# Gate and up products with the weights stationary and the tokens streaming, in the second round of two feed-forwards

## The chip, the cores and the metric

The kernel runs on one core of a Trainium2 chip. The metric is the device time of one execution in microseconds (us); the time of a kernel is the median of its runs. All data is float32 in HBM; 256 tokens with 2048 channels go through one layer of an encoder.

## The reference

One layer has three residual parts: a feed-forward, a mixing part (attention and convolution) and a second feed-forward. Each part normalizes its input, scales and shifts it with vectors computed from a conditioning vector `c` ("modulation"), and normalizes its result again before it is added. What the change touches is the feed-forward:

```python
def swiglu(h, w_gate, w_up, w_down):
    return (jax.nn.silu(h @ w_gate) * (h @ w_up)) @ w_down

h = modulate(rms_norm(x, ffn1_pre_g[l]), sh1, sc1)        # 256 x 2048
f = swiglu(h, ffn1_w_gate[l], ffn1_w_up[l], ffn1_w_down[l])  # 2048 -> 5632 -> 2048
x = x + 0.5 * g1[:, None, :] * rms_norm(f, ffn1_post_g[l])
```

The second feed-forward is the same with its own weights. `mod = c_act @ w_ada + b_ada` gives the nine modulation vectors; `w_ada` alone has 151 MB.

## The kernel before

**Products.** Every operand of a large product is held as two parts of type float32r, a rounded one (hi) and the rest (lo), and a product is three matmuls: hi x hi, hi x lo, lo x hi. A weight chunk is two K tiles (2 x 128 rows) by 512 columns, 512 KB. `wchunk` issues its load on SyncE's queue into one of 7 `raw` buffers, ScalarE casts it to `hi` (L286), VectorE subtracts to get `lo` (L287); `hi` and `lo` have 4 buffers each. The input `hT` is stored transposed, channels on partitions and tokens along the free axis, so that it can be the stationary operand: `Group.products` takes 128 tokens of a K tile as the stationary side and streams 512 weight columns, the result being 128 tokens by 512 columns in one PSUM bank per token tile `t` (L312 to L314).

**Feed-forward.** The 5632 hidden columns are 11 blocks of 512, in two rounds: six blocks, then their share of the down product, then five blocks, then the rest of the down product. The first round (`ffn_start`) has its K tiles in stages, since the modulation is still being computed. The second round (`ffn_rest`, `th` = 1) calls `ffn_up` for each of its five blocks: the gate product `pg` (16 K tiles, 8 chunks), SiLU on ScalarE into `gs` (L446), the up product `pu`, their product `ac` on VectorE (L428). The activations then have their tokens on partitions, but the down product needs them transposed as a stationary operand. So `act_out` turns them: two deferred steps (`turn`, 2 and 3 weight chunks later) each put four 128x128 transposes on TensorE (L385, into a PSUM tile `pa`), a cast on ScalarE (L360) and a subtraction on VectorE (L361) into the two parts of `aT`.

**What sets the order.** The program is written out chunk by chunk: after each chunk's products `tick()` advances the deferred steps and the background lanes (modulation vectors: loads of `w_ada`, multiply-adds on VectorE at L190, transposes `psc` on TensorE at L204). Engines run their queues in order. PSUM has six banks for products (three pairs) and two for transposes. `ffn_down` reads `aT` as the stationary operand, chunk by chunk; the block that comes last is read in the last two of ten chunks.

Of the kernel before, what the change touches and what calls it, by code (L numbers as in the profile page):

```python
# [9 lines left out]
F32 = mybir.dt.float32  # L10
F32R = mybir.dt.float32r
AF = mybir.ActivationFunctionType
# [24 lines left out]
# Chunks over which token tile 0 runs ahead of tile 1 at a part's start and end, and K tiles of  # L37
# tile 0's input that come before the rest.
# [3 lines left out]
# Steps of background work per weight chunk: convolution, modulation in the first feed-forward  # L42
# and in the mixing part.
# [3 lines left out]
# Chunks between an elementwise result and its transposes: rope, activations, conv input.  # L47
# [3 lines left out]
# Buffers for chunks as loaded, and for each of their two parts.  # L51
# [3 lines left out]
# K tiles of the first products of each feed-forward, by stages of their modulation.  # L55
# [5 lines left out]
def encoder_layer(ctx, tc, a, consts, out):  # L61
# [15 lines left out]
    def mm_ps(name):  # L77
        return [psum.tile([P, BLK], F32, tag="mm", name=f"{name}_t{t}") for t in range(NT)]
# [63 lines left out]
    def load_cols(names, i):  # L142
        """Parameter vectors with element j*128+p at [p, j]."""
        rows = work.tile([P, P], F32, tag="rows", name=f"rows{i}")
        at = 0
        for name in names:
            n = a[name].shape[1] // P
            nc.gpsimd.dma_start(rows[at:at + n, :], a[name].rearrange("o (j p) -> (o j) p", p=P))
            pcols[name] = (at, n, i)
            at += n  # L150
        prm = keep.tile([P, sum(a[n].shape[1] for n in names) // P], F32, name=f"prm{i}")
        ps = tr_ps(f"ps_prm{i}")
        nc.tensor.transpose(ps[:, :at], rows[:at, :], ident[:at, :at])
        nc.scalar.copy(prm[:, :at], ps[:, :at])
        pcols[i] = prm
# [12 lines left out]
    def mod_sum(vs, c0, n):  # L168
        """Partial sums over the partitions of columns c0..c0+n of the vectors vs."""
        both = mpool.tile([P, MW], F32, tag="acc", name=f"acc{vs[0]}_{c0}")  # L170
        nc.gpsimd.memset(both, 0.0)
        accs = []
        for m, v in enumerate(vs):
            n0 = v * D + c0
            acc = both[:, m * n:(m + 1) * n]
            nc.gpsimd.dma_start(acc[0:1, :], b_ada[0:1, n0:n0 + n])
            accs.append(acc)
        kt = CH * BLK // n
        for j0 in range(0, NK, kt):
            ws = []  # L180
            for v in vs:
                n0 = v * D + c0
                raw = wpool.tile([P, CH, BLK], F32, tag="raw", bufs=RAW, name=f"ada{v}_{c0}_{j0}")
                w = raw.rearrange("p a b -> p (a b)").rearrange("p (j n) -> p j n", n=n)
                nc.sync.dma_start(w, w_ada[j0 * P:(j0 + kt) * P, n0:n0 + n].rearrange(
                    "(j p) n -> p j n", p=P))
                ws.append(w)
            for j in range(kt):
                for w, acc in zip(ws, accs):
                    nc.vector.scalar_tensor_tensor(acc, w[:, j, :], cact[:, j0 + j:j0 + j + 1], acc,  # L190
                                                   op0=ALU.mult, op1=ALU.add)
            for v in vs:
                yield
        return accs

    def mod_cols(vs, dsts, c0, n):
        """Columns c0..c0+n of the vectors vs with element j*128+p at dst[p, j]."""
# [17 lines left out]
    def mod_affine(vsh, vsc, gname, A, B, c0, n):  # L215
        """A = (1 + scale) * pre gain, B = shift, for columns c0..c0+n."""
# [9 lines left out]
    def mod_gate(v, gname, factor, gc):  # L226
        """gc = factor * vector v * post gain."""
# [4 lines left out]
    def gate_tile(gc, i):  # L232
        """The column vector gc as a row, the same on every partition."""
# [11 lines left out]
    def slot(tag, shape, name, dt=F32):  # L245
        """A tile of at most SLOT elements in a place that several parts use in turn."""
# [29 lines left out]
    def wchunk(w, r0, kt, cols, name):  # L276
        """K tiles from row r0 on, of 512 columns in equal parts from each of cols on."""
# [12 lines left out]
    class Group:  # L290
        """ps[t] (+)= x[t] @ w over K tiles k0..k0+nk and 512 columns; xT holds the K tiles
        from kx on."""
# [23 lines left out]
    def in_step(work):  # L316
        """Chunks of groups, all of token tile 0 before token tile 1."""
# [7 lines left out]
    def group(*args, head=0, tail=0, **kw):  # L325
        """A group, token tile 0 ahead of tile 1 over the first head and the last tail chunks."""
# [10 lines left out]
    def rstd_parts(ssp, n, name, act=False):  # L337
        """(sum of the columns of ssp / n + EPS) ** -0.5"""
# [24 lines left out]
    def pre_norm(hT, dg, A, B, j0, j1, i, t0=0, t1=NT):  # L363
        """K tiles j0..j1 of modulate(rms_norm(x)) transposed, for token tiles t0..t1; dg
        holds 1/rms on diagonals."""
# [15 lines left out]
    def transposed(src, ps, n=2):  # L381
        """[P tokens, t, n*128] -> PSUM [128, n, S]."""
# [17 lines left out]
    def post_add(f, r, i, t):  # L400
        """x += f * r for token tile t, r the rstd of the rows before the gain; returns 1/rms
        of the new rows on a diagonal."""
# [7 lines left out]
    def next_norm(f, ssp, A, B, j1, i):  # L410
        """Residual, and the first j1 K tiles of the next part's input, token tile 0 first over
        the chunks of a group's head."""
# [27 lines left out]

    def ffn_up(aT, slot_i, hT, wg, wu, b, i):
        pg = mm_ps(f"pg{i}_{b}")
        group(pg, hT, wg, 0, NK, b * BLK, f"g{i}_{b}")
        gs = gs_tile(f"{i}_{b}")
        for t in range(NT):
            nc.scalar.activation(gs[:, t, :], pg[t], AF.Silu)  # L446
        pu = mm_ps(f"pu{i}_{b}")
        group(pu, hT, wu, 0, NK, b * BLK, f"u{i}_{b}")
        act_out(aT, slot_i, gs, pu, f"{i}_{b}")
# [16 lines left out]
    def ffn_start(hT, wg, wu, i, stages, mods_of, norm_of, last_lane, begin=None):  # L466
        """Blocks of the first round, K tiles in stages: a stage's modulation is summed up
        while the products of the stage before run."""
# [64 lines left out]
    # ================= first feed-forward =================  # L533
# [35 lines left out]
    def begin2(open_group, run, order):  # L569
        """The first two groups with token tile 0 ahead."""  # L570
# [24 lines left out]
    # ================= attention and convolution =================  # L595
# [42 lines left out]
    def rope_T(pt, name, tag):  # L638
        """PSUM t x [P, 4 heads x 128] -> rotated and transposed [128, head, S]."""
# [26 lines left out]
    def attention(hb, qT, kT):  # L666
        """Heads of one half in overlapping steps: scores, transpose, output."""
# [58 lines left out]
    def attn_parts(hb, hi, lo):  # L726
        """Attention rows times their gain, transposed; 1/rms is applied after the product."""
# [30 lines left out]
    # layer norm over channels, swish: sums over channels on the tensor engine  # L758
# [9 lines left out]
    def rstd_cols(ps, n, name):  # L768
        """Sums of [128 equal rows, S tokens] -> 1/rms with the tokens on partitions."""
# [115 lines left out]
    # ================= second feed-forward =================  # L885
# [67 lines left out]
```

## Time and profile before

| | |
|---|---|
| median of 3 runs | 1992.02 us |
| lowest, highest | 1987.54, 1992.28 us |
| profiled execution, span from first to last instruction | 1997.8 us |
| TensorE busy | 1917.2 us (96%), 8547 matmuls |
| weight loads of TensorE | 1552.7 us (78%) |
| VectorE busy | 1466.7 us (73%) |
| ScalarE busy | 936.7 us (47%) |
| HBM read | 489 MB, 246 GB/s over the span |
| second round, first feed-forward (gate and up) | 465 to 697 us of the span |
| second round, second feed-forward (gate and up) | 1641 to 1871 us of the span |

In the profile's rows, PE is TensorE's matmuls and PEld its loads of stationary operands, ACT is ScalarE, DVE VectorE. `L312` is line 312 of the kernel, which made the instruction. Names are `out<-in`, without buffer numbers; `128*128 128x512` is a matmul with a 128x128 stationary operand and 512 streamed columns. Matmuls are pipelined: the profile's record of one goes on while the next has begun, so the distance between starts says how fast they go. A plain float32 matmul of the program appears as two records.

### The profile page before, as it was taken

The page shows a single profiled execution, that of the slowest core. Times are in us where ns is not written, and L with a number is a line of the kernel's source. Part 1 is how long each engine was busy: PE and PEld are TensorE (multiplying, and loading weights), DVE is VectorE, ACT ScalarE, POOL GpSimd, SP SyncE. Part 2 cuts the span into 40 slices and gives each one's busy share as a digit, 9 for nine tenths or more (in the row PEclk, how much of TensorE's full clock was granted, in tenths as well). Part 3 has the DMA queues.
Part 4 walks back from the last instruction along what each step waited for, and adds up shares of the span by engine and source line. Part 5 has one row for each costly group of instructions (what it writes and reads, how often), then busy time and mean ns, then how long its engine had stood idle before and what let it go on. Part 6 is the DMA issues. An engine that isn't in the chain of part 4 may idle for free.

```text
span 1997.8 us, 23978 instructions
## 1 busy us (share of the span) xinstructions
PE 1917.2 (96%) x8547; PEld 1552.7 (78%) x8547; DVE 1466.7 (73%) x1780; ACT 936.7 (47%) x1439; POOL 65.5 (3%) x90
## 2 busy tenths in 40 slices
PE   2999999999999999899999997999999999999997
PEld 2888888888888877678888786888888777888886
DVE  6789999777777766589997758898776455444454
ACT  3554455444444444644455745635444433444442
POOL 2000000000000000000100000000000000000000
PEclk9999999999999999899999998999999999999999
DMA  9989988999999977356656667998777667656552
GB/s 341 313 296 307 318 266 280 344 320 327 313 318 322 301 251 262 104 176 184 179 167 203 195 205 243 329 325 278 245 224 234 216 231 236 198 180 186 172 189 96
DMA packets 249432, 493.13 MB, mean 247 GB/s; under 512 B 17065, under 2 KB 42433, under 8 KB 249312
## 3 DMA queue, kind: packets, MB, share of 16 engines
q1 hardware_dynamic: 247888, 491.38, 73.8%
q8 instruction: 67, 1.10, 0.2%
q14 instruction: 53, 0.43, 0.1%
q0 software_dynamic: 1248, 0.15, 0.1%
q10 hardware_dynamic: 176, 0.07, 0.0%
HBM read 489.44 MB, written 2.10 MB: 246 GB/s over the span
## 4 chain that ended last, share of the span: by engine, by line
PE 85%; DMA 7%; DVE 4%; issue 2%; ACT 1%; POOL 0%; DVEq 0%; POOLq 0%; ACTq 0%; SPq 0%
PE pg_t L312 8%; PE pg_t L313 8%; PE pg_t L314 8%; PE pu_t L313 8%; PE pu_t L314 7%; PE pu_t L312 7%; DMA ada<-in_w_ada 7%; PE pd_t L313 6%; PE pd_t L314 6%; PE pd_t L312 6%; PE pc_t L312 2%; PE pc_t L313 2%; PE pc_t L314 2%; PE pst L374 1%; DVE lo_d L287 1%
## 5 line engine op out<-in xcount | busy, mean ns | idle before, releaser
L190 DVE SCALAR_TENSOR_TENSOR acc<-ada,cact,acc 128x512 f32<-128x512 f32 (+2 forms) x448 | 394.2, 900 | 148.4 <-DMA ada<-in_w_ada 138.0
L286 ACT CAST hi_d<-raw_d 128x1024 fp32r<-128x1024 f32 x176 | 184.4, 1050 | 273.6 <-PE pd_t L314 233.8
L286 ACT CAST hi_g<-raw_g 128x1024 fp32r<-128x1024 f32 x176 | 184.8, 1051 | 241.4 <-PE pg_t L314 143.8
L287 DVE TENSOR_TENSOR lo_d<-raw_d,hi_d 128x1024 fp32r<-128x1024 f32 x176 | 212.7, 1223 | 111.1 <-ACT hi_d L286 110.7
L286 ACT CAST hi_u<-raw_u 128x1024 fp32r<-128x1024 f32 x176 | 184.7, 1050 | 219.3 <-PE pu_t L314 121.7
L287 DVE TENSOR_TENSOR lo_u<-raw_u,hi_u 128x1024 fp32r<-128x1024 f32 x176 | 214.3, 1223 | 95.9 <-ACT hi_u L286 95.3
L287 DVE TENSOR_TENSOR lo_g<-raw_g,hi_g 128x1024 fp32r<-128x1024 f32 x176 | 214.4, 1223 | 77.1 <-ACT hi_g L286 76.7
L313 PE MATMUL pd_t<-lo_d,a_0h 128*128 128x512 f32 x384 | 152.3, 397 | 4.3 <-DVE lo_d L287 4.2
L312 PE MATMUL pd_t<-hi_d,a_0h 128*128 128x512 f32 x384 | 152.4, 397 | 0.0
L314 PE MATMUL pd_t<-hi_d,a_0l 128*128 128x512 f32 x384 | 151.7, 395 | 0.0
L312 PE MATMUL pg_t<-hi_g,h3h 128*128 128x512 f32 x352 | 141.2, 401 | 1.8 <-ACT h3h L360 1.8
L312 PE MATMUL pg_t<-hi_g,h1h 128*128 128x512 f32 x352 | 140.5, 400 | 0.2 <-ACT h1h L360 0.2
L312 PE MATMUL pu_t<-hi_u,h1h 128*128 128x512 f32 x352 | 140.4, 399 | 0.0
L312 PE MATMUL pu_t<-hi_u,h3h 128*128 128x512 f32 x352 | 140.2, 398 | 0.0
L313 PE MATMUL pg_t<-lo_g,h1h 128*128 128x512 f32 x352 | 139.8, 397 | 0.0
L313 PE MATMUL pg_t<-lo_g,h3h 128*128 128x512 f32 x352 | 139.8, 397 | 0.0
L314 PE MATMUL pg_t<-hi_g,h3l 128*128 128x512 f32 x352 | 139.8, 397 | 0.0
L314 PE MATMUL pg_t<-hi_g,h1l 128*128 128x512 f32 x352 | 139.7, 397 | 0.0
L313 PE MATMUL pu_t<-lo_u,h1h 128*128 128x512 f32 x352 | 139.7, 397 | 0.0
L313 PE MATMUL pu_t<-lo_u,h3h 128*128 128x512 f32 x352 | 139.4, 396 | 0.3 <-DVE lo_u L287 0.3
L314 PE MATMUL pu_t<-hi_u,h3l 128*128 128x512 f32 x352 | 139.4, 396 | 0.0
L314 PE MATMUL pu_t<-hi_u,h1l 128*128 128x512 f32 x352 | 139.2, 396 | 0.0
(258 smaller groups left out, 3631.3 us busy)
## 6 DMA issues: line engine op xcount, KB each, us to landing
ada<-in_w_ada SPq DMA_DIRECT2D x288, 512.0 KB, 5.4
raw_g<-in_ffn_w_gate SPq DMA_DIRECT2D x176, 512.0 KB, 4.9
raw_u<-in_ffn_w_up SPq DMA_DIRECT2D x176, 512.0 KB, 4.9
raw_d<-in_ffn_w_down SPq DMA_DIRECT2D x176, 512.0 KB, 5.3
raw_c<-in_w_in SPq DMA_DIRECT2D x64, 256.0 KB, 3.0
raw_q<-in_w_in SPq DMA_DIRECT2D x16, 512.0 KB, 3.7
raw_k<-in_w_in SPq DMA_DIRECT2D x16, 512.0 KB, 3.7
raw_v<-in_w_in SPq DMA_DIRECT2D x16, 512.0 KB, 3.6
```

The source lines that it names most:

```text
L190: nc.vector.scalar_tensor_tensor(acc, w[:, j, :], cact[:, j0 + j:j0 + j + 1], acc, op0=ALU.mult, op1=ALU.add)
L286: nc.scalar.copy(h, r)
L287: nc.vector.tensor_tensor(l, r, f32(h), op=ALU.subtract)
L312: nc.tensor.matmul(o, xh, h, start=self.first and k == 0, stop=False)
L313: nc.tensor.matmul(o, xh, l, start=False, stop=False)
L314: nc.tensor.matmul(o, xl, h, start=False, stop=self.last and k == self.nk - 1)
L374: nc.tensor.matmul(o[:, (t - t0) * P:(t - t0 + 1) * P], x[:, t, (j + jj) * P:(j + jj + 1) * P], dg[t], start=True, stop=True)
```

## The change

`ffn_up` no longer uses `group` and `act_out`. A new `ColGroup.products` swaps the sides: 128 of the chunk's 512 weight columns are the stationary operand, and the 256 tokens of the transposed input stream past. The result has the hidden columns on partitions and the tokens along the free axis, two pieces of 128 columns to a PSUM bank. SiLU and the product of gate and up keep their shapes, and `ac` is then transposed already: `turn` is only the cast and the subtraction, both two chunks after the block. The products of the first round, the down products and the mixing part are as before. The rest of the diff takes out comments.

```diff
+    class ColGroup(Group):
+        def products(self, c, hl):
+            for j in range(min(CH, self.nk - c * CH)):
+                k = c * CH + j
+                xh, xl = self.xT.h(self.kx + k)[:, 0, :], self.xT.l(self.kx + k)[:, 0, :]
+                for m in range(BLK // P):
+                    o = self.ps[m // 2][:, m % 2 * S:(m % 2 + 1) * S]
+                    ms = slice(m * P, (m + 1) * P)
+                    h, l = hl[0][:, j, ms], hl[1][:, j, ms]
+                    last = self.last and k == self.nk - 1 and m % 2 == 1
+                    nc.tensor.matmul(o, h, xh, start=self.first and k == 0 and m % 2 == 0, stop=False)
+                    nc.tensor.matmul(o, h, xl, start=False, stop=False)
+                    nc.tensor.matmul(o, l, xh, start=False, stop=last)
+
+    def col_group(*args, **kw):
+        g = ColGroup(*args, **kw)
+        for c in range(g.chunks):
+            g.products(c, g.load(c))
+            tick()
+
     def ffn_up(aT, slot_i, hT, wg, wu, b, i):
-        pg = mm_ps(f"pg{i}_{b}")
-        group(pg, hT, wg, 0, NK, b * BLK, f"g{i}_{b}")
-        gs = gs_tile(f"{i}_{b}")
-        for t in range(NT):
-            nc.scalar.activation(gs[:, t, :], pg[t], AF.Silu)
-        pu = mm_ps(f"pu{i}_{b}")
-        group(pu, hT, wu, 0, NK, b * BLK, f"u{i}_{b}")
-        act_out(aT, slot_i, gs, pu, f"{i}_{b}")
+        name = f"{i}_{b}"
+        pg = mm_ps(f"pg{name}")
+        col_group(pg, hT, wg, 0, NK, b * BLK, f"g{name}")
+        gs = gs_tile(name)
+        for n in range(2):
+            nc.scalar.activation(gs[:, n, :], pg[n], AF.Silu)
+        pu = mm_ps(f"pu{name}")
+        col_group(pu, hT, wu, 0, NK, b * BLK, f"u{name}")
+        ac = work.tile([P, NT, BLK], F32, tag="ac", name=f"ac{name}")
+        k0 = 4 * len(aT.hi)
+        aT.add(slot_i)
+        for n in range(2):
+            nc.vector.tensor_tensor(ac[:, n, :], pu[n], gs[:, n, :], op=ALU.mult)
+
+        def turn(n):
+            split_to(aT, k0 + 2 * n, 2, ac[:, n, :].rearrange("p (a s) -> p a s", s=S))
+
+        defer(AD, lambda: turn(0))
+        defer(AD, lambda: turn(1))
```

In the names below, `pg1_6_t0` and `pg1_6_t1` are the two PSUM banks of the gate product of block 6 in the first feed-forward, `hi_g1_6_0` and `lo_g1_6_0` the two parts of its first weight chunk, `h1h0` and `h1l0` those of the input's first four K tiles; the streamed operand stands first behind the arrow.

On TensorE, the first chunk of block 6, before: three matmuls of a K tile for token tile 0 (left out are the chunk's second K tile), then for token tile 1.

```order
L312 MATMUL pg1_6_t0_3775<-hi_g1_6_0_3778,h1h0_232 128x512
L313 MATMUL pg1_6_t0_3775<-lo_g1_6_0_3779,h1h0_232 128x512
L314 MATMUL pg1_6_t0_3775<-hi_g1_6_0_3778,h1l0_233 128x512
...
L312 MATMUL pg1_6_t1_3776<-hi_g1_6_0_3778,h1h0_232 128x512
L313 MATMUL pg1_6_t1_3776<-lo_g1_6_0_3779,h1h0_232 128x512
L314 MATMUL pg1_6_t1_3776<-hi_g1_6_0_3778,h1l0_233 128x512
```

The same place after:

```order
L454 MATMUL pg1_6_t0_3775<-h1h0_232,hi_g1_6_0_3778 128x256
L455 MATMUL pg1_6_t0_3775<-h1l0_233,hi_g1_6_0_3778 128x256
L456 MATMUL pg1_6_t0_3775<-h1h0_232,lo_g1_6_0_3779 128x256
...
L454 MATMUL pg1_6_t1_3776<-h1h0_232,hi_g1_6_0_3778 128x256
L455 MATMUL pg1_6_t1_3776<-h1l0_233,hi_g1_6_0_3778 128x256
L456 MATMUL pg1_6_t1_3776<-h1h0_232,lo_g1_6_0_3779 128x256
```

The left-out rows are now the second 128 columns of the first bank; `t1` holds the third and fourth 128 columns, and the K tile ends after twelve rows instead of six. The rounded weights come in two neighbouring rows as the stationary side, as the rounded input did.

On TensorE, the border between the second and the third chunk of block 7, two chunks behind the end of block 6, before (`pa1_6_0` is the PSUM tile of the first turn, `ac1_6` the activations):

```order
L312 MATMUL pg1_7_t1_4112<-hi_g1_7_1_4135,h1h0_232 128x512
L313 MATMUL pg1_7_t1_4112<-lo_g1_7_1_4136,h1h0_232 128x512
L314 MATMUL pg1_7_t1_4112<-hi_g1_7_1_4135,h1l0_233 128x512
L385 MATMUL pa1_6_0_4152<-ident_73,ac1_6_4106 128x128 x4
L312 MATMUL pg1_7_t0_4111<-hi_g1_7_2_4160,h1h1_234 128x512
L313 MATMUL pg1_7_t0_4111<-lo_g1_7_2_4161,h1h1_234 128x512
L314 MATMUL pg1_7_t0_4111<-hi_g1_7_2_4160,h1l1_235 128x512
```

and after:

```order
L454 MATMUL pg1_7_t1_4304<-h1h0_232,hi_g1_7_1_4339 128x256
L455 MATMUL pg1_7_t1_4304<-h1l0_233,hi_g1_7_1_4339 128x256
L456 MATMUL pg1_7_t1_4304<-h1h0_232,lo_g1_7_1_4340 128x256
L454 MATMUL pg1_7_t0_4303<-h1h1_234,hi_g1_7_2_4373 128x256
L455 MATMUL pg1_7_t0_4303<-h1l1_235,hi_g1_7_2_4373 128x256
L456 MATMUL pg1_7_t0_4303<-h1h1_234,lo_g1_7_2_4374 128x256
```

The four transposes are gone; a second set stood one chunk later.

On ScalarE, the casts of those activations among those of the weight chunks, before:

```order
L286 CAST hi_g1_7_4_4233<-raw_g1_7_4_4232 128x1024
L286 CAST hi_g1_7_5_4251<-raw_g1_7_5_4250 128x1024
L360 CAST a1_1h0_4109<-pa1_6_0_4152 128x512
L286 CAST hi_g1_7_6_4272<-raw_g1_7_6_4271 128x1024
L360 CAST a1_1h0_4109<-pa1_6_1_4177 128x512
```

and after:

```order
L286 CAST hi_g1_7_2_4373<-raw_g1_7_2_4372 128x1024
L286 CAST hi_g1_7_3_4430<-raw_g1_7_3_4429 128x1024
L360 CAST a1_1h0_4299<-ac1_6_4298 128x512 x2
L286 CAST hi_g1_7_4_4463<-raw_g1_7_4_4462 128x1024
L286 CAST hi_g1_7_5_4493<-raw_g1_7_5_4492 128x1024
```

Both casts now read `ac` itself and stand together, ahead of the cast of chunk 4 of block 7.

## Rows read from the trace of the kernel before

**Rows 1.** The page: busy time by engine, granted clock in 40 slices, chain that ended last.

```profile
PE 1917.2 (96%) x8547; PEld 1552.7 (78%) x8547; DVE 1466.7 (73%) x1780; ACT 936.7 (47%) x1439; POOL 65.5 (3%) x90
...
PEclk9999999999999999899999998999999999999999
...
PE 85%; DMA 7%; DVE 4%; issue 2%; ACT 1%; POOL 0%; DVEq 0%; POOLq 0%; ACTq 0%; SPq 0%
```

**Rows 2.** Busy time by stretch: the two second rounds, gate and up products.

```profile
core 0: us, PE busy (x) PEld busy (x) DVE busy (x) ACT busy (x) POOL busy (x), PEclk, DMA share, GB/s
465.20:697.00 231.80, 231.67 (x1034) 188.02 (x1033) 178.78 (x158) 103.51 (x150) 4.32 (x6) 1.00 0.92 315
1641.00:1871.30 230.30, 228.38 (x1001) 184.03 (x1000) 115.40 (x105) 96.13 (x115) 0.00 (x0) 1.00 0.62 200
```

**Rows 3.** Who waited for whom in the first of these stretches: total us, times, longest.

```profile
engine line waited for: us in total, times, longest us
...
ACT hi_g L286 <- PE pg_t L314: 31.9, 19, 1.8
```

**Rows 4.** Instructions in order of time, TensorE, an undisturbed stretch: start, duration.

```profile
545.24 0.39 PE L312 MATMUL pu_t<-hi_u,h1h 128*128 128x512 f32 x1
...
551.54 0.40 PE L312 MATMUL pu_t<-hi_u,h1h 128*128 128x512 f32 x1
```

**Rows 5.** The same view, VectorE: products of gate and up of two neighbouring blocks.

```profile
1779.43 1.28 DVE L428 TENSOR_TENSOR ac<-pu_t,gs 128x512 f32<-128x512 f32 x2
...
1825.09 1.28 DVE L428 TENSOR_TENSOR ac<-pu_t,gs 128x512 f32<-128x512 f32 x2
```

**Rows 6.** The same view, TensorE: one turn of four transposes among the products.

```profile
561.80 0.39 PE L314 MATMUL pg_t<-hi_g,h1l 128*128 128x512 f32 x1
562.04 0.60 PE L385 MATMUL pa<-ident,ac 128*128 128x128 f32 x4
562.39 0.48 PE L312 MATMUL pg_t<-hi_g,h1h 128*128 128x512 f32 x1
562.71 0.39 PE L313 MATMUL pg_t<-lo_g,h1h 128*128 128x512 f32 x1
```

**Rows 7.** The same view, TensorE: plain float32 matmuls of 256 and of 128 columns.

```profile
1018.13 1.02 PE L674 MATMUL pss<-Tk,Tq 128*128 128x256 f32 x4
...
1042.85 1.05 PE L701 MATMUL pso<-v,eT 128*128 128x128 f32 x8
```

**Rows 8.** Groups by line and shape: count, busy us, mean ns of one, idle before.

```profile
L312 PE MATMUL pu_t<-hi_u,h3h 128*128 128x512 f32 x352 | 140.2, 398 | 0.0
...
L312 PEld LDWEIGHTS pu_t<-hi_u,h3h 128*128 128x128 f32 x352 | 66.5, 189 | 15.1
...
L701 PE MATMUL pso<-v,eT 128*128 128x128 f32 x64 | 8.5, 277 | 0.5 <-ACT eT L694 0.5
L701 PEld LDWEIGHTS pso<-v,eT 128*128 128x128 f32 x64 | 8.2, 191 | 1.3 <-ACT eT L694 0.8
L674 PE MATMUL pss<-Tk,Tq 128*128 128x256 f32 x32 | 8.2, 379 | 0.0
```

**Rows 9.** A stretch at half the clock: by stretch, and TensorE's instructions in it.

```profile
1214.20:1217.20 3.00, 3.00 (x8) 2.34 (x7) 3.00 (x7) 2.04 (x7) 0.00 (x0) 0.50 0.19 44
...
1214.28 0.63 PE L313 MATMUL pg_t<-lo_g,h3h 128*128 128x512 f32 x1
...
1216.84 0.63 PE L312 MATMUL pg_t<-hi_g,h3h 128*128 128x512 f32 x1
```

**Rows 10.** Groups by line and shape: casts on ScalarE from SBUF and from PSUM.

```profile
L360 ACT CAST h1h<-hf 128x512 fp32r<-128x512 f32 x8 | 5.0, 622 | 0.2
...
L360 ACT CAST a_1h<-pa 128x512 fp32r<-128x512 f32 x20 | 11.6, 579 | 1.4 <-PE pa L385 1.4
```

## The prediction

> **What bounds the kernel now.** I read the page first. TensorE is busy 96% of the span and carries 85% of the chain that ended last [rows 1], so the whole program is bound by TensorE unless a stage says otherwise. The reader is to see the granted clock too: 9 tenths or more in nearly every slice, so the stage that changes runs at the full 2.4 GHz. Second, the table by stretch for the two places that change, the second rounds of the feed-forwards [rows 2]. TensorE is busy 231.67 of 231.80 us in the first and 228.38 of 230.30 us in the second; VectorE is at 77% and 50%, the DMA engines at 92% and 62%, and the clock is 1.00. What is idle on TensorE is 2 us of 462. Third, who waits for whom there: ScalarE's cast of the next weight chunk waits for TensorE to give its buffer back [rows 3], not the other way round. So in these 460 us what TensorE needs for its instructions is the time, and I cost the change by the distance between the starts of two neighbouring matmuls. (The busy times of single matmuls can't be added: they overlap, 0.39 us long at a distance of 0.23.)
>
> That distance: from the first to the last row of [rows 4] there are 27 steps in 6.30 us, 233 ns a matmul of 512 columns. A whole block agrees: two products of a gate block and its successor lie 45.66 us apart [rows 5], with 192 matmuls and two turns of 0.44 us (below) in it, so (45.66 - 0.88) / 192 = 233 ns.
>
> **The change part by part.** *Transposes.* Each of the ten changed blocks (five per feed-forward) loses two turns of four transposes. What one turn costs TensorE stands in [rows 6]: from the matmul at 561.80 to the one at 562.71 pass 0.91 us, with two ordinary steps of 0.233 in it, so a turn is 0.44 us. (The matmul behind the transposes starts early, 0.03 us after the last of them, and gives it back in the longer step behind it.) It lies on the path, since TensorE is the bound. 20 turns x 0.44 = **-8.9 us**.
>
> *Matmuls.* Per block, chunk and K tile, six matmuls of 512 columns become twelve of 256. The streamed columns stay the same, 3072; the number of matmuls, and of stationary loads, doubles. 2 x 5 x 2 x 16 x 6 = 1920 matmuls go, 1920 x 233 ns = -447.4 us; 3840 come. Everything hangs on their distance T, which no row of before shows, since the kernel has no product of this type under 512 columns. Sum: 3840 T - 447.4 - 8.9, and it is zero at T = 118.8 ns.
>
> The bound below: the plain float32 matmuls of 128x128 each bring a load of their own and stand (1.05 - 0.277) / 7 = 0.111 us apart; those of 256 columns (1.02 - 0.379) / 3 = 0.214 us [rows 7, 8]. These take two passes a column: the step between the two forms is 103 ns for 128 columns, where 128 x 2 / 2.4 GHz = 106.7. So a float32 matmul of 128 columns streams as long as one of the new ones would at full rate, with an equal load beside it (191 against 189 ns [rows 8]), and 111 ns is the nearest row from below. The load is almost wholly hidden there: 8 ns at most is left over the streaming.
>
> The bound above: 512 columns at 2.4 GHz are 213 ns, and the float32 rows with the same streaming time really stand 214 apart, but the kernel's own products stand 233 apart. If these 19 ns belong to the instruction and not to its columns, T = 107 + 19 = 126 ns.
>
> Which end is nearer? Two rows speak for the columns. With the same nominal streaming, the record of one product matmul is 398 ns long and that of the 256-column float32 one 379 [rows 8]: the 19 ns lie inside the record, between first and last column, not between two records. And at half the clock the surplus is gone: in [rows 9] the granted clock is 0.50, and six steps take 2.56 us, 427 ns, which is 512 / 1.2 GHz to the nanosecond. A fixed cost at each start would be there too; columns that arrive a little slower than the array at full speed can take them would not be seen. That the surplus is not the load's is in [rows 6]: the step from 561.80 to 562.04 has a transpose's load in it and is no shorter. So I take T near half of 233, 116.5, and half a nanosecond for what does not halve: **T = 117 ns**, 3840 x 117 = 449.3 us, +1.9 against before. Both ends are kept: 111 gives -21.1 and 126 gives +36.4 on this term.
>
> The Trainium skill, "TensorE: Matmul & The Clock Gate", section "Back-to-back issue gap", gives N / 2.4 + 2.5 ns for a lone matmul: 216 at 512 columns, 109 at 256. The trace disagrees at 512 (233), so the measurement decides; with 233 before and the page's 109 after, the sum would be 3840 x 0.109 - 456.3 = -38 us.
>
> *What moves and costs nothing.* The cast of an activation now reads SBUF and not PSUM: 622 ns instead of 579 [rows 10], 20 casts, 0.9 us on ScalarE, which is 42 to 45% busy in these stretches [rows 2]; if that cover were gone it would cost the 0.9. SiLU and product keep their shapes (128x512). The two halves of a block now end 0.7 us apart instead of 1.4, so ScalarE waits a little longer in front of the first SiLU; behind it in its queue stand casts of chunks, and those wait for TensorE already [rows 3]. The activations come two weight chunks after the block, one earlier for the second half, and the first down product that reads them is eight chunks away. The weights are now the stationary side, so where a chunk is late its load stands in front of the matmul too; TensorE's idle time in [rows 2] leaves 2 us for that. DMA: the chunks and their issues are the same in number and order.
>
> *Sum.* +1.9 - 8.9 = **-7.0 us** on the profiled execution, whose span from first to last instruction is 1997.8 us; that is already 0.3% over the median of 1992.02 of the runs without a profile, and I take the difference over unchanged: **1985 us**.
>
> **Rivals.** *A fixed cost per matmul* (slower): the 19 ns are charged for each instruction. T = 126, 3840 x 0.126 - 456.3 = +27.5 us, 2020. For it: nothing in the trace shows a product of another width; the half clock could hide a fixed cost that runs beside the array. Against it: the longer records and [rows 6]. It decides from T = 118.8 on. A like result comes if loads that follow each other without a pause (189 ns long each, one every 117) or the instruction stream get in each other's way: the trace has such a density only for eight matmuls in a row [rows 7], not for 45 us.
>
> *The load sets the pace* (faster): the surplus vanishes when TensorE streams 256 columns at a time and only the load is left, T = 111: 3840 x 0.111 - 456.3 = -30 us, 1962. For it: the rows at 111. Against it: the surplus sits in the stream.
>
> *Loads that are not hidden* (much slower): if each extra load stood alone, 1920 x 111 ns = +213 us, 2196 with the transposes off. The 8 ns left in the float32 rows speak against it; these already have a new load for every 128 columns. The same page of the Trainium skill, section "The mechanism" of its Part 3, says that a load overlaps running matmuls only when the row group differs; here every operand takes all 128 rows, so by that rule the loads would stand in line. The trace disagrees: 111 ns for streaming and load together.
>
> *The change doesn't do what it says*: the order of instructions has twelve 256-column matmuls and no transposes there, so this is left with the case that TensorE was not the bound; then the time stays at 1992. With 2 us idle in 462 it is unlikely.
>
> **How the numbers follow.** Surplus by columns, T 115 to 119: 0.52, times from 1977 to 1993, predicted 1985. Load sets the pace, T under 115: 0.14, 1962 to 1977. Fixed cost or crowding, T 119 to 129: 0.26, 1993 to 2031. Loads in line: 0.03. No effect: 0.05. The range 1966 to 2018 leaves out the last few us of the fast case (0.04) and the upper part of the slow ones (0.11 with the loads in line). The case of the columns alone has 1977 to 1993. 0.3% is 6 us, about what a measurement of this kernel can tell from no change: faster by more is under 1986, T below 117.3, which is the fast case and some 0.3 of the middle one, 0.45; within 0.3% up to 1998 (T up to 120.4), the rest of the middle case, no effect, and a little of the slow one, 0.28; slower 0.27.
>
> **What would show it.** In the second rounds: starts of the new matmuls 117 ns apart (116 to 118) with records of some 287 ns (the float32 row of equal streaming has 277, and half of 19 is added; 296 if the surplus is fixed); a block 45 us long (384 x 0.117 = 44.9) instead of 45.7; no transposes of activations there; TensorE still busy nearly all the time, the clock at 1.00, VectorE and ScalarE as before. Steps of 126 ns and blocks of 48.4 us would show the fixed cost; steps of 111 ns with loads back to back, the load's pace; idle time on TensorE in these stretches that was not there before, a late chunk, which none of these terms holds. The rest of the program should not move.

## The result, and the profile after

The changed kernel takes 2003.59 us (median of 4 runs, 2003.13 to 2005.02) against 1992.15 us for the kernel before (1987.54 to 1995.61): 1.0062 times as long, 95% interval 1.0048 to 1.0076, or about 12 us more. The forecast was 1985. The profiled execution of the changed kernel spans 2001.8 us, that of before 1997.8; the spans are 4 us apart, since the one of before was taken in one of its longer executions, so I compare stretches of the two traces and take totals from the times.

The page of the changed kernel, the lines that answer to [rows 1] (busy time by engine, granted clock, chain that ended last):

```profile
PE 1920.8 (96%) x10387; PEld 1645.4 (82%) x10387; DVE 1468.0 (73%) x1780; ACT 938.2 (47%) x1439; POOL 63.8 (3%) x90
...
PEclk9999999999999999899999998999999999999999
...
PE 87%; DMA 6%; DVE 4%; issue 1%; ACT 1%; POOL 0%; DVEq 0%; POOLq 0%; ACTq 0%; SPq 0%
```

The page hardly differs: the engines are as busy as before, and that is why it doesn't tell where 12 us went. Two views do. Whom TensorE waited for between 465 and 760 us (the first feed-forward's second round and the start of its down products), before and then after; columns: total us, times, longest:

```profile
PE pd_t L313 <- DVE lo_d L287: 3.3, 2, 2.7
```

```profile
PE psg L239 <- ACT G1h L241: 7.4, 1, 7.4
PE pg_t L456 <- DVE lo_g L287: 3.4, 1, 3.4
```

TensorE now waits 10.8 us where it waited 3.3. What this adds up to is read from the down products that follow, the first rows of `pd` that use the new activations (duration shortest/median/longest in ns, first and last start), before and then after:

```profile
L312 PE MATMUL pd_t<-hi_d,a_1h x160: 390/394/483, 698.6 to 817.5; 128*128 128x512 f32 x160
```

```profile
L312 PE MATMUL pd_t<-hi_d,a_1h x160: 390/393/774, 714.2 to 827.7; 128*128 128x512 f32 x160
```

They start 15.6 us later and end 10.2 us later, since the kernel before loses some time within them. So the loss is made before 714 us. And the table by stretch (busy us of each engine, granted clock, DMA share, GB/s) in two parts of the second round, before and then after:

```profile
465.00:600.00 135.00, 134.87 (x597) 109.38 (x596) 104.21 (x92) 60.44 (x90) 2.88 (x4) 1.00 0.92 318
600.00:700.00 100.00, 100.00 (x459) 81.61 (x458) 77.02 (x69) 44.80 (x62) 1.44 (x2) 1.00 0.92 311
```

```profile
465.00:600.00 135.00, 135.00 (x1135) 135.00 (x1134) 104.38 (x92) 60.91 (x90) 2.89 (x4) 1.00 0.93 318
600.00:700.00 100.00, 96.55 (x794) 96.34 (x793) 67.83 (x62) 41.10 (x57) 1.44 (x2) 0.97 0.85 282
```

Up to 600 us the two kernels move the same 318 GB/s. From there the changed one falls to 282, where before had 311 with TensorE never idle. Loads of w_ada (rows of the modulation's weights, for the background sums) share the seven buffers, and SP's queue, with the weight chunks; whom VectorE waited for between 600 and 730 us, before and then after:

```profile
DVE acc L190 <- DMA ada<-in_w_ada: 20.0, 14, 5.2
DVE lo_u L287 <- ACT hi_u L286: 8.2, 10, 2.1
DVE lo_g L287 <- ACT hi_g L286: 5.8, 10, 1.6
```

```profile
DVE acc L190 <- DMA ada<-in_w_ada: 40.4, 25, 3.0
DVE lo_d L287 <- ACT hi_d L286: 3.8, 1, 3.8
```

Before, VectorE ran ahead and waited, in part, for ScalarE's casts; after, it waits 25 times for a w_ada load, 40 us in all.

**One of these waits, engine by engine.** The order of VectorE's instructions in the changed kernel, at block 10 of the first feed-forward (built by the framework's scheduler; `acc` is a modulation sum, `ada` the buffer with a w_ada load, `lo` the second part of a weight chunk `raw`):

```
DVE  lo_g1_10_2 <- raw_g1_10_2
DVE  ac1_9 (two products)
DVE  acc5_0 <- ada5_0_6
DVE  a1_1l3 <- ac1_9
DVE  lo_g1_10_3 <- raw_g1_10_3
DVE  lo_g1_10_4 <- raw_g1_10_4
```

and the order in which SP issues the loads, here the same in both kernels (over the whole program one load, of convolution weights, comes three places earlier after the change): raw_g1_10_3, 4, ada5_0_4, raw_g1_10_5, ada5_0_5, raw_g1_10_6, 7, **ada5_0_6**, raw_u1_10_0. So the sum over ada5_0_6 stands ahead of the `lo` of five chunks (3 to 7) whose loads were issued before its own. In the kernel before, the sum that stands behind lo_g1_10_2 is the one over ada5_0_4, ahead of two earlier loads (3 and 4). Counted through the second round, a sum stands ahead of mostly one earlier chunk load in blocks 6 and 7, one or two in 8, two in 9 and two, then three in 10 before the change; after it, of one in block 6, one to three in 7, mostly three in 8 and four in 9 and 10 (once five). In the down products behind the round it is three to four in the kernel before too, and there its 3.3 us of waits stand.

In the changed kernel's trace, VectorE, SP's queue, ScalarE and TensorE around that instruction (instructions in order of time: start, duration, then the wait in front):

```profile
655.42 1.28 DVE L477 TENSOR_TENSOR ac<-pu_t,gs 128x512 f32<-128x512 f32 x2
659.22 1.28 DVE L190 SCALAR_TENSOR_TENSOR acc<-ada,cact,acc 128x1024 f32<-128x1024 f32 x1 [2.52 <-DMA ada<-in_w_ada]
660.42 1.29 DVE L361 TENSOR_TENSOR a_1l<-ac,a_1h 128x512 fp32r<-128x512 f32 x2
661.62 2.35 DVE L287 TENSOR_TENSOR lo_g<-raw_g,hi_g 128x1024 fp32r<-128x1024 f32 x2
```

```profile
651.82 1.50 SPq L284 DMA_DIRECT2D raw_g<-in_ffn_w_gate  x2
654.39 0.34 SPq L185 DMA_DIRECT2D ada<-in_w_ada  x1
655.53 0.37 SPq L284 DMA_DIRECT2D raw_u<-in_ffn_w_up  x1
660.53 0.34 SPq L185 DMA_DIRECT2D ada<-in_w_ada  x1
```

```profile
656.14 1.22 ACT L360 CAST a_1h<-ac 128x512 fp32r<-128x512 f32 x2 [4.22 <-DVE ac L477]
657.26 2.94 ACT L286 CAST hi_g<-raw_g 128x1024 fp32r<-128x1024 f32 x3
```

```profile
659.17 0.28 PE L455 MATMUL pg_t<-h1l,hi_g 128*128 128x256 f32 x1
662.89 0.58 PE L456 MATMUL pg_t<-h1h,lo_g 128*128 128x256 f32 x1 [3.45 <-DVE lo_g L287]
663.27 0.41 PE L454 MATMUL pg_t<-h1h,hi_g 128*128 128x256 f32 x1
```

The load of ada5_0_6 is issued at 654.39, and VectorE is through with everything ahead of its sum at 656.7; it stands until 659.2. Meanwhile chunks 3 to 7 keep five of the seven buffers, ada5_0_6 and raw_u1_10_0 have the other two, and SP, whose next load needs a buffer, issues nothing from 655.9 to 660.53, until the sum ends at 660.50. So the next w_ada load is late as well. TensorE waits for lo of chunk 3 until 662.89 and then comes back at half the clock: from 663.27 to 667.97 22 steps take 4.70 us, 213 ns each, 2.1 us more than at the 119 ns found further down. From 668.3 on the granted clock is 1.00 again (the last of these rows, then the table by stretch):

```profile
667.97 0.41 PE L455 MATMUL pg_t<-h1l,hi_g 128*128 128x256 f32 x1
```

```profile
663.30:668.00 4.70, 4.70 (x24) 4.70 (x24) 3.10 (x3) 0.18 (x1) 0.00 (x0) 0.50 0.87 285
668.30:674.00 5.70, 5.70 (x50) 5.70 (x49) 3.56 (x3) 1.85 (x3) 0.00 (x0) 1.00 0.81 274
```

ScalarE is drawn in too. Its cast of the activations waited 4.22 us for the late `ac`, with weight casts behind it. The 7.4 us at 705 us are the same cast of the last block, with the copy G1h, for which TensorE waited, behind it; and its `ac` stands on VectorE behind a sum that waits for its load (ScalarE, then VectorE):

```profile
703.26 0.59 ACT L241 COPY G1h<-psg 128x512 f32<-128x512 f32 x1
711.27 0.62 ACT L360 CAST a_1h<-ac 128x512 fp32r<-128x512 f32 x1 [7.43 <-DVE ac L477]
711.80 0.58 ACT L241 COPY G1h<-psg 128x512 f32<-128x512 f32 x1
```

```profile
709.35 1.28 DVE L190 SCALAR_TENSOR_TENSOR acc<-ada,cact,acc 128x1024 f32<-128x1024 f32 x1 [2.48 <-DMA ada<-in_w_ada]
710.56 1.28 DVE L477 TENSOR_TENSOR ac<-pu_t,gs 128x512 f32<-128x512 f32 x2
```

**The distance of the new products.** TensorE in a dense stretch of the changed kernel, the first and the last of 21 rows:

```profile
559.99 0.28 PE L456 MATMUL pg_t<-h1h,lo_g 128*128 128x256 f32 x1
...
562.37 0.28 PE L455 MATMUL pg_t<-h1l,hi_g 128*128 128x256 f32 x1
```

20 steps in 2.38 us are 119 ns; the forecast had 117, and break-even is 118.8. Two neighbouring blocks of the second feed-forward, the rows that answer to [rows 5]:

```profile
1785.30 1.40 DVE L477 TENSOR_TENSOR ac<-pu_t,gs 128x512 f32<-128x512 f32 x2
...
1830.87 1.40 DVE L477 TENSOR_TENSOR ac<-pu_t,gs 128x512 f32<-128x512 f32 x2
```

A block takes 45.57 us, or 118.7 ns for each of its 384 products, where it took 45.66: the change gains a tenth of a microsecond there and not the 0.7 forecast. The records are 0.28 us long, close to the 287 ns that the surplus by columns gave (296 if it were fixed).

### The profile page after: what moved, and what is told of

Read it like the earlier page. It is cut to its first block, busy times and chain, and to the rows that moved or that the text cites. A ratio compares the mean times of both kernels' runs of the same rounds, so it can differ in the third digit from the quotient of the medians.

```text
span 2001.8 us, 27646 instructions
## 1 busy us (share of the span) xinstructions
PE 1920.8 (96%) x10387; PEld 1645.4 (82%) x10387; DVE 1468.0 (73%) x1780; ACT 938.2 (47%) x1439; POOL 63.8 (3%) x90
## 4 chain that ended last, share of the span: by engine, by line
PE 87%; DMA 6%; DVE 4%; issue 1%; ACT 1%; POOL 0%; DVEq 0%; POOLq 0%; ACTq 0%; SPq 0%
PE pd_t L313 8%; PE pd_t L312 8%; PE pd_t L314 8%; DMA ada<-in_w_ada 6%; PE pg_t L312 5%; PE pg_t L313 5%; PE pg_t L314 5%; PE pu_t L313 4%; PE pu_t L314 4%; PE pu_t L312 4%; PE pg_t L455 3%; PE pg_t L456 3%; PE pg_t L454 3%; PE pu_t L456 3%; PE pu_t L455 3%; PE pu_t L454 3%
## 5 line engine op out<-in xcount | busy, mean ns | idle before, releaser
L287 DVE TENSOR_TENSOR lo_d<-raw_d,hi_d 128x1024 fp32r<-128x1024 f32 x176 | 213.0, 1223 | 119.2 <-ACT hi_d L286 118.7
L312 PE MATMUL pd_t<-hi_d,a_1h 128*128 128x512 f32 x320 | 127.2, 397 | 0.0
L313 PE MATMUL pd_t<-lo_d,a_1h 128*128 128x512 f32 x320 | 126.5, 395 | 0.0
L314 PE MATMUL pd_t<-hi_d,a_1l 128*128 128x512 f32 x320 | 126.5, 395 | 0.0
L456 PE MATMUL pg_t<-h1h,lo_g 128*128 128x256 f32 x320 | 91.6, 286 | 3.4 <-DVE lo_g L287 3.4
L455 PE MATMUL pg_t<-h1l,hi_g 128*128 128x256 f32 x320 | 91.3, 285 | 0.0
L454 PE MATMUL pg_t<-h1h,hi_g 128*128 128x256 f32 x320 | 91.2, 285 | 0.0
L456 PE MATMUL pg_t<-h3h,lo_g 128*128 128x256 f32 x320 | 90.5, 283 | 0.0
L455 PE MATMUL pg_t<-h3l,hi_g 128*128 128x256 f32 x320 | 90.4, 282 | 0.0
L456 PE MATMUL pu_t<-h3h,lo_u 128*128 128x256 f32 x320 | 90.4, 282 | 0.0
L456 PE MATMUL pu_t<-h1h,lo_u 128*128 128x256 f32 x320 | 90.3, 282 | 0.0
```

What stands on the lines that cost most here:

```text
L287: nc.vector.tensor_tensor(l, r, f32(h), op=ALU.subtract)
L312: nc.tensor.matmul(o, xh, h, start=self.first and k == 0, stop=False)
L313: nc.tensor.matmul(o, xh, l, start=False, stop=False)
L314: nc.tensor.matmul(o, xl, h, start=False, stop=self.last and k == self.nk - 1)
L454: nc.tensor.matmul(o, h, xh, start=self.first and k == 0 and m % 2 == 0, stop=False)
L455: nc.tensor.matmul(o, h, xl, start=False, stop=False)
```

## The experiments

Three theories. **A**: the products themselves, 119 instead of 117 ns, make the loss. **B**: ScalarE's place behind a late `ac`. **C**: VectorE's order, sums ahead of earlier chunks, starves the loads. C came up while the first four runs were read; they were made for A and B.

**One feed-forward at a time.** The new block code is used in one feed-forward, the old in the other: `if i == 2` in the first run, `if i == 1` in the second.

> The change made in the second feed-forward's second round alone; the first feed-forward is as before. Theory B: no modulation loads run beside VectorE there, ac is never late, so the time is that of the kernel before or a little under it, 1989 to 1993 us. Theory A with products as the whole loss: half of it, 1997 to 1999 us.

> The change made in the first feed-forward's second round alone; the second feed-forward is as before. Theory B: the whole loss stands here, 2002 to 2006 us. Theory A with products as the whole loss: half of it, 1997 to 1999 us.

Second alone: 1992.07 us, ratio to before 0.9999 (0.9989 to 1.0009). First alone: 2008.44 us, 1.0086 (1.0071 to 1.0101). So the loss is wholly in the first feed-forward, though both have the same number of products; A as the whole loss is out. What sets the first apart are the w_ada loads: 58 are issued in its second round, while only six sums over such loads stand at the start of the other's. Those six stand ahead of five earlier chunk loads each, in both kernels alike. In the changed kernel VectorE waits 24.6 us for their loads, the DMA share is 0.71 (1647 to 1698 us), and TensorE does not wait at all from 1647 to 1877 us. So the order by itself costs nothing where such loads are few and the DMA engines have room.

The first alone came out 2 us above what B expected, and some 5 us above the full change (the intervals just overlap). The order on every engine is the same as in the full change up to the end of the first feed-forward. TensorE's waits from 465 to 760 us add up to 14.6 us against 10.8, the longest 9.0 us at the same G1h, which is most of the 5; why they come out longer was not settled.

**ScalarE freed.** In the changed kernel the cast of the activations, which `split_to` gives to ScalarE, goes to VectorE:

```diff
-            split_to(aT, k0 + 2 * n, 2, ac[:, n, :].rearrange("p (a s) -> p a s", s=S))
+            src = ac[:, n, :].rearrange("p (a s) -> p a s", s=S)
+            hi, lo = aT.h(k0 + 2 * n, 2), aT.l(k0 + 2 * n, 2)
+            nc.vector.tensor_copy(hi, src)
+            nc.vector.tensor_tensor(lo, src, f32(hi), op=ALU.subtract)
```

> The changed kernel with one edit: the rounding of each block's activations to float32r (a_h from ac) is done by VectorE right behind the ac product instead of by ScalarE. Theory B (the loss is a new wait: ScalarE's in-order queue stands at that cast until a late ac, and TensorE then waits for the weight casts and G1h copies behind it): the 3.7 and 7.6 us waits of TensorE in the first feed-forward's second round go, and the median falls from 2003.6 to 1991 to 1996 us. Theory A (the loss is in the 256-column products themselves, 119 us per 1000 instead of the 117 forecast, with the waits only incidental): stays at 2002 to 2005, since no product is touched. A third case: VectorE, 73% busy, becomes late by the 40 added casts of some 0.3 to 0.6 us each: 2005 to 2015.

1999.64 us, ratio 1.0043 (1.0028 to 1.0058): about a third of the loss is gone, with an interval that overlaps that of the full change. That lies between what A and B expected and is neither's; the added casts are 20, not the 40 of the expectation. TensorE's waits from 465 to 760 us moved:

```profile
PE pd_t L313 <- DVE lo_d L287: 7.2, 4, 4.8
PE pu_t L456 <- DVE lo_u L287: 2.5, 3, 2.0
PE pg_t L456 <- DVE lo_g L287: 0.3, 1, 0.3
```

The 7.4 us for G1h are gone, and 10.0 us of waits stand there all the same, now for VectorE, which still waits 39.9 us for w_ada loads from 600 to 730 us. B is where a late VectorE shows, not why it is late.

**Width alone.** The kernel before, with transposes and casts as they were, issues the three products of a K tile in the second rounds on 256 of the 512 columns, then on the other 256 (`...` stands for a line left out):

```diff
+                for m in range(2):
+                    ms = slice(m * 256, (m + 1) * 256)
+                    o = self.ps[t][:, ms]
+                    h, l = hl[0][:, j, ms], hl[1][:, j, ms]
+                    ...
+                    nc.tensor.matmul(o, xh, h, start=self.first and k == 0 and m == 0, stop=False)
+                    nc.tensor.matmul(o, xh, l, start=False, stop=False)
+                    nc.tensor.matmul(o, xl, h, start=False, stop=last)
```

> The kernel before with one edit: each 512-column product of the second rounds is issued as two of 256 columns with the same activations stationary, one half of the columns after the other; transposes, casts and activation layout stay as before. So only the instruction size is tested, 3840 products of 256 columns in place of 1920 of 512. Theory A (a 256-column product takes about 119 ns, 2.5 over half of 233): 3840 x 2.5 ns = +9.8, so 2001 to 2003 us against 1992. If the size costs only the 0.5 ns each that the prediction took: +1.9, 1994 us. If loads denser by two do not hide at all: 2100 us and more.

2013.26 us, 1.0111 (1.0095 to 1.0128), 20 us over before, twice what A allowed. Its VectorE order has moved as well (sums ahead of two to three earlier loads in block 7 and of four or five from the end of block 8 on); VectorE waits 48.1 us for w_ada loads, and the DMA engines move 277 GB/s from 600 to 700 us. The width of the instruction is enough to make the scheduler reorder VectorE.

**VectorE's order fixed.** In the changed kernel, in the halves version and in the kernel before, each sum from the first feed-forward's second round to the end of its down products (there `behind[0]` is set) is tied behind the `lo` of the chunk loaded last (`...` stands for lines left out):

```diff
+            ck = cact[:, j0:j0 + kt]
+            if behind[0]:
+                ck = work.tile([P, kt], F32, tag="ck", bufs=4, name=f"ck{vs[0]}_{c0}_{j0}")
+                nc.vector.scalar_tensor_tensor(ck, f32(los[-1])[:, 0, :kt], 0.0, cact[:, j0:j0 + kt],
+                                               op0=ALU.mult, op1=ALU.add)
             ...
-                    nc.vector.scalar_tensor_tensor(acc, w[:, j, :], cact[:, j0 + j:j0 + j + 1], acc,
+                    nc.vector.scalar_tensor_tensor(acc, w[:, j, :], ck[:, j:j + 1], acc,
```

> The changed kernel with one edit, from the second round of the first feed-forward on to its end: each modulation multiply-add of VectorE (acc, from ada) is tied behind the weight part lo of the chunk loaded before it, by a tiny VectorE instruction that makes its coefficient column from that part (some 60 added instructions). In the changed kernel a multiply-add stands ahead of the parts of 2 to 5 chunks whose loads were issued before its own; here of none. Theory C (the loss is this order: VectorE waits for the newest load while landed chunks keep their buffers, so the loads fall behind): VectorE's wait for ada loads in 600 to 730 us falls from 40 us to under 20, the waits of TensorE go, median 1984 to 1994 us. Theory B (only ScalarE's place behind ac): little change, 1999 to 2003. Theory A (products): 2002 to 2006.

> The kernel before with the same edit to the multiply-adds (there they stand ahead of 1 to 3 chunks in the second round and of 4 in the down products behind it). Theory C: the little that the kernel before loses there (TensorE waits of some 6 us between 696 and 770 us) goes in part, 1985 to 1992 us. If the order matters only with the change: 1991 to 1994 us. With this order in both, the difference of the changed kernel to this one is the change's own sum: by 119 ns for a 256-column product and the transposes gone, 9.8 - 8.9 = about +1 us; by the prediction's 117 ns -7 us.

> The kernel before with its second-round products issued as two halves of 256 columns, and the same edit to the multiply-adds. Against the kernel before with that edit alone it is the price of the instruction size alone, with the order of VectorE's work held equal: by 119 ns a product 3840 x 2.5 ns = +9.8 us, by the prediction's 117 ns +1.9 us; if the whole loss of the unpinned version of this kernel (+20 us) were the size, +20 us.

| | as scheduled | tied | ratio of tied to before |
|---|---|---|---|
| changed kernel | 2003.59 | 1987.74 | 0.9981 (0.9970 to 0.9992) |
| before | 1992.15 | 1987.84 | 0.9986 (0.9975 to 0.9997) |
| before, halves | 2013.26 | 1996.44 | 1.0024 (1.0013 to 1.0035) |

With the order fixed the changed kernel loses nothing: it has no wait of TensorE at all between 465 and 760 us, VectorE none for w_ada from 600 to 730, and the table by stretch of the tied changed kernel reads

```profile
465.00:600.00 135.00, 135.00 (x1134) 134.93 (x1133) 109.84 (x125) 60.76 (x90) 2.89 (x4) 1.00 0.91 311
600.00:700.00 100.00, 100.00 (x845) 99.79 (x844) 83.19 (x94) 45.08 (x63) 1.44 (x2) 1.00 0.92 315
```

315 GB/s where the untied one had 282. C holds, and the kernel before paid a little of the same price. The tie moves little besides VectorE's sums: the load of convolution weights goes further forward; and in the changed kernel, at the start of the down products, one cast of activations and one copy G1h change places on ScalarE, and two products come ahead of eight transposes on TensorE. In ratios: the order costs the changed kernel 0.81% (16 us) and the kernel before 0.14% (3 us); the difference, 13 us, is the measured 12 within the intervals.

What remains is the change's own sum: 1987.74 against 1987.84, nothing. The size alone, halves against before with both tied, is +8.6 us, 8.6 / 3840 = 2.2 ns a product. The blocks say the same. ScalarE's SiLUs of the gate (times, first and last start) over the first feed-forward's second round, in the tied changed kernel, the tied kernel before and the tied halves:

```profile
L478 ACT ACTIVATE gs<-pg_t x10: 587/595/599, 487.8 to 674.6; 128x512 f32<-128x512 f32 x10
```

```profile
L454 ACT ACTIVATE gs<-pg_t x10: 597/598/601, 485.3 to 671.9; 128x512 f32<-128x512 f32 x10
```

```profile
L469 ACT ACTIVATE gs<-pg_t x10: 597/598/603, 484.8 to 675.5; 128x512 f32<-128x512 f32 x10
```

186.8, 186.6 and 190.7 us: 1536 products in place of 768 cost 4.1 us (2.7 ns for each of the 1536), and the eight turns of transposes saved, 8 x 0.44 = 3.5, give it back.

**How far behind.** The same tie to the `lo` one chunk earlier (`los[-2]`), so that a sum stands ahead of one earlier load.

> The changed kernel with the multiply-adds tied one chunk earlier: behind the weight part of the chunk before the last one loaded, so that each stands ahead of one earlier load instead of none. Theory C: close to the version that is tied behind the last chunk, 1984 to 1996 us, not above it by more than 3 us, since six of seven buffers still can be in flight. If any multiply-add ahead of an earlier load is as bad as four: 2000 us and more.

1987.01 us, 0.9981 (0.9970 to 0.9992): no worse. One landed chunk behind a sum costs nothing, and with two to three in blocks 9 and 10 of the kernel before TensorE did not wait; four cost, in this stretch with the DMA engines at 92%.

**Buffers.** `RAW = 6` in place of 7, in the changed kernel and in its tied version.

> The changed kernel with six buffers for loaded chunks in place of seven, nothing else. Theory C (multiply-adds ahead of 3 to 4 earlier loads keep that many landed chunks in their buffers, so only the rest are in flight): two to three are left in flight, the loads fall behind earlier and further, 2025 to 2060 us. If the waits come from the multiply-adds' place alone and buffers are no part of it: 2003 to 2008.

> The changed kernel with the multiply-adds tied behind the last loaded part, and six buffers in place of seven. Theory C: with no landed chunk kept behind a multiply-add five or six loads can be in flight, so the loss against the same kernel with seven buffers (1987.7) is small in the first feed-forward; other parts of the program, whose order is not tied, lose some: 1990 to 2010 us, and 15 us or more below the untied kernel with six. If buffers as such are what is short: the same loss as the untied kernel has.

Untied 2015.28 us, 1.0126 (1.0111 to 1.0141); tied 1993.93, 1.0004 (0.9990 to 1.0018). The missing buffer costs 12 to 13 us untied and 5 to 6 tied: the direction and the gap of 21 us that C gave, though the untied loss is smaller than the 2025 us expected at least (with six buffers the scheduler puts the sums of blocks 9 and 10 mostly ahead of three earlier loads, not four). The buffers held behind the sums are part of the mechanism.

**What makes 119 ns.** From the tied changed kernel, in the products between the first and last K tile:

```diff
+                    if 0 < k < self.nk - 1 and self.name[1] == "1":
+                        h, l, o = h[:, :64], l[:, :64], o[:64]
+                    if 0 < k < self.nk - 1 and self.name[1] == "2":
+                        o, xh, xl = o[:, :192], xh[:, :192], xl[:, :192]
```

> A probe of one product's time, from the version with the multiply-adds tied; it leaves work out. In the first feed-forward's second round the K tiles between the first and the last load only 64 of each 128 weight columns (half the load, 256 tokens streamed as before); in the second feed-forward's second round they load all 128 and stream 192 of the 256 tokens. Starts of successive products in dense stretches: if a product costs a fixed 5.4 ns and 0.444 ns for each token, the first stay at 119 ns and the second fall to about 91 ns. If the weight load sets part of the 119: the first fall to 116 to 117 and the second stop at the load's own pace, some 107 to 111 ns.

Its TensorE rows, 64 columns loaded (first and last of 19), then 192 tokens streamed (first and last of 21):

```profile
560.30 0.28 PE L467 MATMUL pg_t<-h1l,hi_g 128*64 128x256 f32 x1
...
562.40 0.28 PE L467 MATMUL pg_t<-h1l,hi_g 128*64 128x256 f32 x1
```

```profile
1702.69 0.27 PE L466 MATMUL pu_t<-h3h,hi_u 128*128 128x192 f32 x1
...
1704.93 0.27 PE L468 MATMUL pu_t<-h3h,lo_u 128*128 128x192 f32 x1
```

2.10 / 18 = 116.7 ns with half the load, just half of the 233 of [rows 4]; 2.24 / 20 = 112 ns with a quarter fewer tokens, where the stream alone would be some 88 (three quarters of 116.7). So the stream of 256 tokens takes what the prediction said, by columns, and the rest of the 119 is the full load, which with a load at every product runs at a pace of 112 ns (just over the 107 to 111 expected) and is not quite hidden at 117. Half the load is also half the output columns; the two were not told apart, but the 112 ns stand without that.

## Why the prediction was wrong, by its steps

The sum was -7 us, and two of its steps failed: the term for the matmuls is 6.7 us too low, and the order of the engines that move, put at nothing, cost some 13 us more than in the kernel before. -7 + 6.7 + 13 = 12.7, the 12 us measured within the intervals. That the time lies in the range, and in the span of the rival "fixed cost or crowding", is luck: by the prediction's formula it needs T = 122 ns, and T was 119.

*What bounds the kernel* held: where TensorE doesn't wait, its distance of starts is the time. But [rows 2] was read as a table of one engine. A DMA share of 0.92 over 230 us was in it, which leaves little room for loads that start late; the argument took from it only that TensorE was not waiting now.

*Transposes*, -8.9: held by the size of the blocks (3.5 us for eight turns closes the sum of the tied kernels).

*Matmuls*: the surplus of 19 ns is by columns, as argued, and the rivals' T of 126 and of 111 ns are out. The term was mis-sized: half a nanosecond "for what does not halve" should have been 2.2, and 3840 x 2.2 is +8.6 us measured, not +1.9. The step that failed is the reading of "8 ns at most is left over the streaming" in the rows at 111 ns (worked out again, (1.05 - 0.277) / 7 is 110): the probe's 112 ns, with 88 of streaming, say that the load and not the stream is the pace of such rows. With this term right the sum would have been 8.6 - 8.9 = -0.3: "within 0.3%", and that is what the two tied kernels show. The Trainium skill's 109 ns ("TensorE: Matmul & The Clock Gate", "Back-to-back issue gap") is further off than the rows: 119 were measured. The same page of the Trainium skill has the rule ("The mechanism" of Part 3) that a load overlaps only a matmul of another row group, which would give the load and the stream in line, while 112 and 116.7 ns give 119 together.

*What moves and costs nothing* failed, and its 13 us are the whole of the loss. The text said "the chunks and their issues are the same in number and order", which is true of SP but for one load of convolution weights, and looked at the moved rows of TensorE and ScalarE; VectorE's order, which the scheduler also moved, by one or two places of the sums, was not looked at. Its sums came to stand ahead of four earlier loads, and TensorE waited 10.8 us where it had waited 3.3. The cover named for the casts, ScalarE's 42 to 45% of busy time, is a share and no cover against a queue in which a cast stands for 7 us behind a late product. The sign to look for was named ("idle time on TensorE in these stretches that was not there before, a late chunk, which none of these terms holds"), but it had no price and no chance of its own; the rivals were, but for that of no effect, all prices of one matmul.

Of the signs: records of 0.28 us, no transposes and full clock in dense stretches came out; 45 us a block did not (45.57), and idle time came in the first feed-forward.

The best version that ran is either kernel with the sums tied: 0.1 to 0.2% under the kernel before, and the layout makes no difference to it.

## What to carry to other kernels

Where a scheduler sets the order, a change of one engine's instruction size can reorder another engine: compare the order on every engine that frees a shared buffer, and count for each consumer how many older loads it stands ahead of. A ring of buffers with R slots has only R minus that number for loads in flight. With the DMA engines at 92%, four of seven kept back took the rate from 315 to 282 GB/s; with six such sums and the DMA engines at 71%, five kept back cost TensorE nothing. A one-instruction dependency that puts consumers in the order of their loads is cheap insurance. And when a stationary load comes with every product, look for a row in which the load, not the stream, is the pace before calling it hidden.

## What the runs showed of the hardware

- A 128-column load with every product runs at 112 ns a product when 192 float32r tokens are streamed behind it, and adds 2 ns to products of 256 tokens that take 116.7 ns with half the load.
- After 3.7 us without a product TensorE came back at half the clock: the next 22 steps took 213 ns each, which is 256 / 1.2 GHz, and cost 2.1 us more than at 119 ns, on top of the wait itself.
